# A two-layer hybrid attention encoder on one core: steps recorded and sorted by a list pass in the kernel, one set of places, and float32 value products in runs

## The chip, the core and the metric

The kernel runs on one core of one Trainium2 chip. The core has five engines, each with a queue of its own that runs in order: TensorE (PE in the profile, with its weight loads as PEld), VectorE (DVE), ScalarE (ACT), GpSimd (POOL) and SyncE (SP), which here issues nearly all transfers. They meet through semaphores. Working memory is SBUF (128 partitions), matmuls write the eight banks of PSUM, and tensors lie in HBM. The metric is the device time of one execution in microseconds (us); less is better.

## The reference, cut to what matters

One sequence of 1,024 tokens with 1,024 features, float32, goes through two layers. Each layer has four attention groups side by side, a joint output projection and an MLP:

```python
for l in range(DEPTH):                                  # DEPTH = 2
    h = rms_norm(x, norm1_g[l])
    proj = h @ w_in[l]
    ...
    y_a = mla_mixer(...)     # 4 heads, latent, dense, 96-wide scores
    y_b = diff_mixer(...)    # 4 heads, softmax(s0) - lam * softmax(s1), dense
    y_c = swa_mixer(...)     # 4 heads, +-128 band with a sink
    y_d = na_mixer(...)      # 4 heads, 2-D neighbourhood on a 64-wide grid, bias
    mix = jnp.concatenate([rms_norm(y_a, ...), y_b, rms_norm(y_c, ...), rms_norm(y_d, ...)], axis=-1)
    x = x + mix @ w_out[l]
    h = rms_norm(x, norm2_g[l])
    x = x + jnp.square(jax.nn.relu(h @ w_up[l])) @ w_down[l]
return rms_norm(x, final_norm_g)
```

## The kernel before

Activations are kept transposed (features on partitions, tokens along the free axis). A product in float32 accuracy is made of three passes of the type float32r: a value is split into a high and a low part (`split`: ACT copies the high part, DVE subtracts it), and `passes` (L222, L223, L224) multiplies high by high, high by low and low by high, 512 columns each. The MLP uses a seven-product scheme for 2 x 2 blocks, so that its matmul count is 7/8 of the plain one.

**One layer, in order.** (1) `several` projects the first tiles of group B, then the second wave; the evacuations rotate (rope), split and store queries, keys and values in HBM (`emit_parts`, `to_values`). (2) Group B's dense attention (`attn_b`, `dense`, `softmax`) runs on 128 queries at a time: scores in two halves of 512 keys (L810), a reduction by DVE that negates and takes the minimum (L812), the exponential by ACT (L815). The second softmax is scaled by ACT (L898) and added by POOL (L190, `p<-p`). The result is transposed by PE in blocks of 128 x 128 (L846) and copied out of PSUM as a split pair: ACT writes `pth` (L196), DVE writes `ptl` (L190). The value product then takes values stored as 64 high and 64 low columns, and multiplies them with `pth` and with `ptl` (L834, L835), 256 queries wide; `pv_out` adds the two halves. Meanwhile the other projections are woven in. (3) Groups D and C (`attn_d`, `attn_c`, `banded`: L982 scores, L991 transposes, L1003 and L1004 value products) run head by head, with the latent up-projections of group A (`latent_up`) woven in. (4) Group A (`attn_a`, `dense`), with a first part of the output projection woven in. (5) The rest of the output projection, then `mlp_up` and `mlp_down`. In between, `tails` holds the short chains that end a head: reciprocal, transpose to rows, store to HBM, a broadcast load back (`rz`), a multiplication.

**What sets the order.** In attention the order of a queue comes from the framework's scheduler, which goes by the order of the code and by priorities (`weave`, `high_priority`); in the MLP PE's order is that of the code. Memory comes from pools with so many buffers per tag: `stack` tiles (queries and keys of a head, L810 and L982) share 8 places with the residual `x`, the bias has 1, values have 2. PSUM banks are divided anew for attention (mm 2, tr 2, sb 3, pv 1), the output projection and the MLP.

Of the kernel before, what the change touches and what calls it, by code (L numbers as in the profile page):

```python
# [14 lines left out]
F = mybir.dt.float32  # L15
# [85 lines left out]
def layout(i):  # L101

    def padded(a, axis):
# [9 lines left out]
    wo = i["w_out"].reshape(n, 8, P, DM)[:, [2, 3, 6, 7, 4, 5, 0, 1]].reshape(n, DM, DM)  # L113
# [23 lines left out]
        + [col(i["out_g_" + s]) for s in ("mla", "swa", "na")]  # L137
# [9 lines left out]

class Trunk:
    def __init__(self, ctx, tc, d, out):
        self.ctx, self.tc, self.nc, self.d, self.out = ctx, tc, tc.nc, d, out  # L150
        self.ahead, self.tails = 4, deque()
        pool = lambda **k: ctx.enter_context(tc.tile_pool(**k))
        self.const = pool(name="const", bufs=1)
        self.xp = pool(name="xp", bufs=8)
        self.big = pool(name="big", bufs=16)
        self.wp = pool(name="wp", bufs=3)
        self.cp = pool(name="cols", bufs=2)
        self.dram = pool(name="dram", bufs=1, space=bass.MemoryType.DRAM)


# [10 lines left out]
    @contextmanager  # L171
    def banks(self, **n):

        self.phase = getattr(self, "phase", 0) + 1
        with self.tc.tile_pool(name=f"ps{self.phase}", bufs=1, space=bass.MemoryType.PSUM,
                               reuse_waits="tile") as self.psum:
            self.nbanks = n
            yield

    def bank(self, tag, shape=(P, 512)):  # L180
        return self.psum.tile(list(shape), F, tag=tag, bufs=self.nbanks[tag], name=tag)
# [87 lines left out]
    def rows_of(self, col, grid=False):  # L269
# [6 lines left out]
        dr = self.dram.tile([n, P], F, tag="rows", bufs=4, name="drows")  # L276
        if grid:
            flat = dr.rearrange("a b -> (a b)").rearrange("(r b c) -> b r c", r=16, b=8)
            self.store(flat, sb.rearrange("b (r c) -> b r c", r=16))
# [23 lines left out]
    def setup(self):  # L303
        nc, d = self.nc, self.d
        tile = lambda shape, name, dt=F: self.const.tile(shape, dt, name=name)
# [75 lines left out]
    def attention(self, l):  # L381
        nc, tc, d = self.nc, self.tc, self.d
        rb = self.rb
        sbuf = lambda name, side="left": tc.tile_pool(name=f"{name}{l}", bufs=1, reuse_waits="tile", side=side)
        w_in = lambda t: d["w_in"][l, t]
        dr = lambda shape, name: self.dram.tile(shape, F, tag=name, bufs=1, name=name)
# [3 lines left out]
        qb, kb, vb = dr([2, 2, 4, 16, 2, S], "qb"), dr([2, 2, 4, 16, 2, S], "kb"), dr([4, P, 8, P], "vb")  # L390
# [1108 lines left out]
```

## Time and profile before

| | us |
|---|---|
| median of 3 runs | 2693.91 |
| lowest, highest | 2693.65, 2694.74 |
| the profiled execution | 2692.41 |
| its span, first to last instruction | 2690.6 |
| granted TensorE clock, mean | 0.971 of full |

The profile is of one execution. Its page gives the busy time of each engine; a group's row gives line, engine, operation, tiles and shapes, count, busy time and mean nanoseconds of one, then the engine's idle time ahead of it and what ended that. A view by windows cuts the span into stretches, and the chain of waits follows the last instruction back to what released it. A matmul's row lasts from its entry to the modelled end of its way through the array, so rows overlap. A plain float32 matmul stands as two records (40 of L299 in the program, 80 in the trace).

### The profile page before, as it was taken

What the parts mean: (1) busy time and instruction counts of PE and PEld (TensorE: products, weight loads), DVE (VectorE), ACT (ScalarE), POOL (GpSimd) and SP (SyncE); (2) the same over time, 40 slices, a digit from 0 to 9 for tenths busy, and PEclk for the clock granted to TensorE, in tenths of its full rate; (3) what the DMA queues carried; (4) which work ended last, traced back from release to release, by engine and by line L of the source; (5) the groups of instructions that cost most, each with busy time, mean ns of one, the idle gap of its engine ahead of it and who ended that gap; (6) DMA issues with size and microseconds to landing.
All of it is one profiled execution on the core that took longest, in us unless ns stands there. A gap on an engine that the chain in (4) does not pass through costs nothing.

```text
span 2690.6 us, 36835 instructions
## 1 busy us (share of the span) xinstructions
PE 2545.8 (95%) x12296; PEld 2107.6 (78%) x12296; DVE 2014.2 (75%) x3827; ACT 1442.9 (54%) x2601; POOL 496.9 (18%) x306
## 2 busy tenths in 40 slices
PE   8989988999899999999999999789998999999997
PEld 7778876787778887888877788678887788778886
DVE  6777867774977778888668777677749677788886
ACT  4667757664534444444437777576635344444444
POOL 2555642201000000000035556331010000000000
PEclk9999989999999999999999999889999999999998
DMA  5533598322144447444244446962221444664431
GB/s 169 177 106 123 160 282 254 83 88 60 51 154 143 161 162 269 146 141 141 96 136 140 121 118 174 306 200 70 70 71 61 152 152 151 227 221 150 132 102 63
DMA packets 186927, 389.15 MB, mean 145 GB/s; under 512 B 23712, under 2 KB 26736, under 8 KB 186736
## 3 DMA queue, kind: packets, MB, share of 16 engines
q1 hardware_dynamic: 172912, 361.62, 43.7%
q10 hardware_dynamic: 13824, 25.17, 2.6%
q8 instruction: 97, 1.59, 0.2%
q14 instruction: 94, 0.77, 0.1%
HBM read 263.29 MB, written 123.41 MB: 144 GB/s over the span
## 4 chain that ended last, share of the span: by engine, by line
PE 74%; DVE 12%; DMA 6%; ACT 4%; issue 3%; POOL 1%; SPq 0%; DVEq 0%; ACTq 0%; POOLq 0%
PE u L222 8%; PE u L224 8%; PE u L223 8%; PE mm L222 5%; PE mm L223 5%; PE mm L224 5%; PE p L222 5%; PE p L223 5%; PE p L224 5%; PE sb L810 3%; PE tr L846 2%; DVE p L812 2%; DVE part L190 2%; PE pv L835 2%; PE pv L834 2%
## 5 line engine op out<-in xcount | busy, mean ns | idle before, releaser
L196 ACT ACTIVATE wh<-raw 128x512 fp32r<-128x512 f32 x448 | 281.8, 630 | 595.9 <-PE u L223 336.0
L190 DVE TENSOR_TENSOR wl<-raw,wh 128x512 fp32r<-128x512 f32 x448 | 306.8, 685 | 76.9 <-ACT wh L196 75.6
L190 POOL TENSOR_TENSOR wl<-ws,wh 128x512 fp32r<-128x512 f32 (+1 forms) x112 | 146.5, 1310 | 1107.0 <-DMA saved<-x 664.1
L224 PE MATMUL u<-far,wl 128*128 128x512 f32 x768 | 302.4, 394 | 6.2 <-DVE wl L190 6.0
L222 PE MATMUL u<-far,wh 128*128 128x512 f32 x768 | 302.4, 394 | 3.3 <-ACT ev L1251 2.1
L223 PE MATMUL u<-far,wh 128*128 128x512 f32 x768 | 301.8, 393 | 0.9 <-DVE far L190 0.9
L190 DVE TENSOR_TENSOR ptl<-tr,pth 128x512 fp32r<-128x512 f32 (+2 forms) x384 | 238.3, 629 | 67.5 <-ACT pth L196 65.8
L815 ACT ACTIVATE p<-p,nm 128x1024 f32<-128x1024 f32 x192 | 220.1, 1147 | 91.1 <-DVE nm L812 89.6
L196 ACT ACTIVATE pth<-tr 128x512 fp32r<-128x512 f32 (+2 forms) x384 | 204.9, 546 | 104.4 <-PE tr L846 55.8
L222 PE MATMUL p<-far,wh 128*128 128x512 f32 x640 | 251.2, 393 | 2.6 <-DVE ev L190 2.6
L224 PE MATMUL p<-far,wl 128*128 128x512 f32 x640 | 250.0, 391 | 2.9 <-DVE wl L190 2.9
L223 PE MATMUL p<-far,wh 128*128 128x512 f32 x640 | 250.3, 391 | 0.0
L810 PE MATMUL sb<-stack 96*128 96x512 f32 x640 | 217.6, 421 | 18.8 <-DVE nm L812 17.8
L190 POOL TENSOR_TENSOR p<-p 128x1024 f32<-128x1024 f32 x64 | 154.0, 2410 | 141.4 <-ACT p L898 132.1
L190 DVE TENSOR_TENSOR raw<-raw 128x512 f32<-128x512 f32 x256 | 174.6, 686 | 6.7 <-DMA raw<-in_w_up 2.0
L224 PEld LDWEIGHTS u<-far,wl 128*128 128x128 f32 x768 | 145.8, 190 | 38.4 <-DVE wl L190 7.9
L222 PEld LDWEIGHTS u<-far,wh 128*128 128x128 f32 x768 | 146.1, 190 | 35.3 <-ACT ev L1251 2.9
L223 PEld LDWEIGHTS u<-far,wh 128*128 128x128 f32 x768 | 145.8, 190 | 31.9 <-DVE far L190 1.6
L222 PE MATMUL mm<-xh,wh 128*128 128x512 f32 x416 | 168.9, 406 | 1.3 <-DVE part L190 0.7
L812 DVE CUSTOM_DVE_ANT_0 p<-sb,zero,nm 128x512 f32<-128x512 f32 x192 | 142.4, 742 | 32.2 <-PE sb L810 28.6
L224 PE MATMUL mm<-xh,wl 128*128 128x512 f32 x416 | 166.5, 400 | 0.0
L223 PE MATMUL mm<-xl,wh 128*128 128x512 f32 x416 | 166.4, 400 | 0.0
(245 smaller groups left out, 5993.1 us busy)
## 6 DMA issues: line engine op xcount, KB each, us to landing
act<-acts SPq DMA_DIRECT2D x224, 256.0 KB
raw<-in_w_up SPq DMA_DIRECT2D x128, 256.0 KB
acts<-ev SPq DMA_DIRECT2D x128, 256.0 KB
raw<-in_w_down SPq DMA_DIRECT2D x128, 256.0 KB
acts<-ev ACTq DMA_DIRECT2D x96, 256.0 KB
ws<-in_w_in SPq DMA_DIRECT2D x76, 256.0 KB
rz<-drows SPq DMA_DIRECT2D x40, 256.0 KB
stack<-kd SPq DMA_DIRECT2D x32, 256.0 KB
```

The costliest lines, as they stand in the source:

```text
L190: (eng or self.nc.vector).tensor_tensor(out=out, in0=a, in1=b, op=op)
L196: nc.scalar.activation(hi, src, AF.Copy)
L222: mm(ps, w[0], x[0][:, sl], start=start, stop=False)
L223: mm(ps, w[0], x[1][:, sl], start=False, stop=False)
L224: mm(ps, w[1], x[0][:, sl], start=False, stop=stop)
L810: self.nc.tensor.matmul(ps, q[:, qt * P:(qt + 1) * P], k[:, sl], start=i == 0, stop=i == len(passes) - 1)
L812: self.nc.vector.tensor_tensor_reduce(out=p[:, sl], in0=ps, in1=self.zero[:, 0:1].bitcast(F).broadcast_to([P, 512]), scale=-scale, scalar= ...
L815: self.nc.scalar.activation(p, p, AF.Exp, bias=nm[:, 1:2], scale=-1.0, accum_out=z)
L834: nc.tensor.matmul(out, v[:, kt], h[:, sl], start=kt == 0, stop=False)
L835: nc.tensor.matmul(out, v[:, kt], lo[:, sl], start=False, stop=kt == 7)
L846: nc.tensor.transpose(t[:, k * 256 + i * P:k * 256 + (i + 1) * P], p[:, (j * 2 + k) * P:(j * 2 + k + 1) * P], self.ident)
```

## The change

Four things change together.

**Recording and sorting.** The kernel's `nc` is now a `Plan`: each call is recorded as a `Step`, with the tiles that it reads and writes as `View`s of `Cell`s. A stage's steps get a rank by a table (`SPAN`), spread over a stretch from start to end; `order` then walks all five queues with a price for each step (`price`), takes on each queue the ready step of lowest rank whose tiles find a place (`grant`, `place`), and `emit` issues all steps in that order, with the framework's order switched off on every engine. So all instructions have one source line, L648.

**One set of places.** SBUF is 40 places of 1,024 columns, 19 of 512, and small ones; PSUM is 8 banks. Any tile takes any free place of its size, under a cap per tag: stack 12, bias 3, values 5, transposed tiles 8, and for banks mm 8, tr 3, sb 4, pv 2.

**Value products in float32.** Values are stored as 64 plain columns (half the bytes). The transposed block is copied once, unsplit, into `pt`: by ACT in group B, by ACT and DVE in turn in D, C and A. The product is a float32 matmul with 64 columns of weights. In `dense` the two key blocks of a pair go to partitions 0 to 63 and 64 to 127 of the bank, and `pv_out` adds them; in `banded` the two go to the two heads of a pair, which now run side by side, and one copy evacuates both. The products of a block are one unit (`together`), issued as a run. Group C's heads are paired differently, and the weights' rows are laid out to suit.

**Group B's difference** is one DVE instruction instead of one by ACT and one by POOL. The first wave's evacuations read PSUM without a copy by ACT.

The diff, cut to what the prediction speaks of:

```diff
+class Plan:
+    def order(self):
...
+            for s in pick.steps:
+                free[n] = self.issue(s, max(t, free[n]))
...
+        return sorted(out, key=lambda s: (s.start, s.n))
...
+    def place(self, c, t):
+        k, coming = c.kind, self.coming[c.kind]
+        rank = bisect.bisect_left(coming[c.tag], c.rank)
+        if rank >= c.cap - self.live[k, c.tag]:
+            return False
...
+    PLACES = {"pair": 40, "half": 19, "row": 3, "col": 30, "bank": 8}
...
+    def emit(self):
+        real = lambda v: v.real() if isinstance(v, View) else v
+        steps = self.plan.order()
+        for c in self.plan.cells:
+            c.home = self.home
+        with self.tc.manual_schedule(engines={q.engine.engine for q in self.plan.queues.values()}):
+            for s in steps:
+                getattr(s.eng.engine, s.op)(*[real(a) for a in s.args], **{k: real(a) for k, a in s.kw.items()})
...
-    EV = (.5, .5, .7, 1)
-    EARLY, RC, RA, LA = 4, (8, 1), (3, 1), 0
+    SPAN = {"open": (0, 60), "b1": (62, 95), "lat": (95, 130), "pd": (130, 210), "pc": (210, 300), "b": (65, 300),
+            "d": (300, 400), "up": (300, 370), "c": (305, 405), "a": (405, 510), "mb": (330, 335), "md": (405, 410),
+            "mc": (415, 420), "ma": (515, 520), "o1": (505, 530), "o2": (530, 600), "mlp": (600, 1220)}
+    LAYER, SOON = 1250, 20
+    BANKS = {"mm": 8, "tr": 3, "sb": 4, "pv": 2}
...
     def to_values(self, dst, tag="mm"):
...
-            nc.scalar.activation(v[..., 0:64], src, AF.Copy)
-            self.tt(v[..., 64:128], src, v.bitcast(F)[..., 0:64], ALU.subtract)
...
+            nc.scalar.activation(v.rearrange("p (h k d) -> p h k d", h=2, k=4),
+                                 ps.rearrange("p (k h d) -> p h k d", k=4, h=2), AF.Copy)
...
-    def transposed(self, w):
-        return [self.ap.tile([P, 512], R, tag=n, bufs=3, name=n)[:, :w] for n in ("pth", "ptl")]
+    def transposed(self, ps):
+        t = self.place.tile([P, 512], F, tag="pt", bufs=self.NT, name="pt")[:, :ps.shape[1]]
+        if self.turns[0]:
+            self.nc.vector.tensor_copy(t, ps)
+        else:
+            self.nc.scalar.activation(t, ps, AF.Copy)
+        self.turns = self.turns[::-1]
+        return t
...
-                nc.tensor.matmul(out, v[:, kt], h[:, sl], start=kt == 0, stop=False)
-                nc.tensor.matmul(out, v[:, kt], lo[:, sl], start=False, stop=kt == 7)
...
+            with self.plan.together():
+                for n, j in enumerate((3, 2, 1, 0)):
+                    for k in range(2):
+                        nc.tensor.matmul(out[k * 64:(k + 1) * 64], v[:, j * 2 + k], pts[j][:, k * 256:k * 256 + 256],
+                                         start=n == 0, stop=n == 3)
...
-                nc.scalar.activation(ps[1], ps[1], AF.Copy, scale=c)
-                self.tt(ps[0], ps[0], ps[1], ALU.add, nc.gpsimd)
+                nc.vector.scalar_tensor_tensor(out=ps[0], in0=ps[1], scalar=c, in1=ps[0], op0=ALU.mult, op1=ALU.add)
...
+        def products(pv, half, kbs):
+            with self.plan.together():
+                for kb in kbs:
+                    pts, i0, i1 = done[kb]
+                    q0, q1 = max(i0, half * 4), min(i1, half * 4 + 3) + 1
+                    for r, v, pt in zip(heads, vs, pts):
+                        mm(pv[r, (q0 - half * 4) * P:(q1 - half * 4) * P], v[:, kb],
+                           pt[:, (q0 - i0) * P:(q1 - i0) * P], start=False, stop=kb == 2 + 3 * half)
```

How it moves instructions, at two places. First PE in group A of the first layer (`sb` and the later `bank` rows with `stack` are scores, `ident,p` transposes, `pv` or `pt,v` value products; xN means N in a row). Before:

```order
L834 MATMUL pv<-pth,v 128x256
L810 MATMUL sb<-stack 128x512 x3
L835 MATMUL pv<-ptl,v 128x256
L834 MATMUL pv<-pth,v 128x256
L835 MATMUL pv<-ptl,v 128x256
L846 MATMUL tr<-ident,p 128x128 x4
L810 MATMUL sb<-stack 128x512 x3
L834 MATMUL pv<-pth,v 128x256
L835 MATMUL pv<-ptl,v 128x256
```

The change, same engine and group:

```order
L648 MATMUL bank_107<-stack 128x512 x3
L648 MATMUL bank_103<-stack 128x512 x3
L648 MATMUL bank_105<-ident,p 128x128 x2
L648 MATMUL bank_102<-ident,p 128x128 x2
L648 MATMUL bank_101<-pt,v 64x256 x8
L648 MATMUL bank_105<-ident,p 128x128 x2
L648 MATMUL bank_102<-ident,p 128x128 x2
L648 MATMUL bank_104<-stack 128x512 x3
```

A block's value products stood in pairs between transposes and scores, each behind its own split; now eight of one block stand in a run, some steps after their transposes.

Second, SP from group C's first key store on, ahead of the band stage (groups D and C) of the first layer: `kd`, `qd` and `vd` are group D's keys, queries and values in HBM, `kc` and `qc` group C's keys and queries, `rq`, `rkv` and `latp` group A's latent tiles. Before:

```order
L169 DMA kc<-both 64x2x512 x2
L162 DMA stack<-kd 64x1024 x2
L162 DMA stack<-qd 64x1024
L162 DMA bias<-in_bias 128x768
L162 DMA stack<-kd 64x1024
L162 DMA stack<-qd 64x1024
L162 DMA stack<-kd 64x1024
L162 DMA rq<-drows 128x1024
L162 DMA rkv<-drows 128x1024
L162 DMA latp<-lat 128x1024 x2
```

The change:

```order
L648 DMA kc_126<-both 64x2x512 x2
L648 DMA v<-vd_124 128x512
L648 DMA stack<-kd_123 64x1024 x2
L648 DMA v<-vd_124 128x512
L648 DMA tabc<-in_c 128x1024
L648 DMA tabs<-in_s 128x1024
L648 DMA ws<-in_w_lat 128x512
L648 DMA stack<-qc_125 64x1024 x2
L648 DMA kc_126<-both 64x2x512 x2
L648 DMA stack<-qc_125 64x1024 x2
L648 DMA mask<-in_swa 128x384
L648 DMA rq<-drows_134 128x1024
```

Before, the loads of group D's later heads stood here, and group C's came behind the latent tiles. Now group D's first pair is complete here, group C's queries come next, and group D's second pair stands behind the latent tiles. From this store to the last load of group A's first head 31 MB pass through SP's queue before, and 30 MB now.

More of the change, by code (lines that the diff above doesn't have):

```diff
@@ L867, in dense @@
             step(job, j)
-        product(*ready.pop(0))
+        while runs:
+            products()
         yield True
```

1020 lines of the change are left out of this document (685 added, 335 removed).

## The prediction, made before the changed kernel ran

> **What bounds the kernel now.** I read the page's totals first, then one stretch in which TensorE (PE) runs undisturbed, then the same view cut into stages, then the chain of waits inside the worst stage.
>
> ```profile
> span 2690.6 us, 36835 instructions
> ## 1 busy us (share of the span) xinstructions
> PE 2545.8 (95%) x12296; PEld 2107.6 (78%) x12296; DVE 2014.2 (75%) x3827; ACT 1442.9 (54%) x2601; POOL 496.9 (18%) x306
> ```
>
> PE looks 95% busy, but a matmul's row is its whole way through the array, and the next starts long before it ends. So busy time hides slack, and pace shows it:
>
> ```profile
> 1100.00:1200.00 100.00, 100.00 (x443) 82.84 (x442) 85.66 (x139) 44.21 (x74) 0.00 (x0) 1.00 0.46 140
> ```
>
> 443 matmuls of 512 columns in 100 us are 0.227 us each (0.226 to 0.227): the full pace. Starts in the timeline give the other prices:
>
> ```profile
> 612.51 0.28 PE L834 MATMUL pv<-pth,v 128*128 128x256 f32 x1
> 612.63 0.28 PE L835 MATMUL pv<-ptl,v 128*128 128x256 f32 x1
> 612.75 0.27 PE L846 MATMUL tr<-ident,p 128*128 128x128 f32 x1
> ...
> 186.35 1.04 PE L846 MATMUL tr<-ident,p 128*128 128x128 f32 x8
> 187.15 0.47 PE L810 MATMUL sb<-stack 96*128 96x512 f32 x1
> ```
>
> A split-float32 (fp32r) matmul of 256 columns takes 0.12 (612.51 to 612.63), a 384-column one 0.174 by interpolation (an estimate), a transpose 0.10 to 0.11 (8 from 186.35 to 187.15). Now the stages: two attentions (four rows each) and two MLPs. A row reads: stretch, length, PE busy (x matmuls), PEld, DVE, ACT, POOL, granted clock, DMA share, GB/s.
>
> ```profile
> 0.00:84.00 84.00, 74.35 (x326) 61.01 (x327) 54.72 (x70) 35.66 (x54) 24.82 (x22) 0.98 0.60 193
> 84.00:330.00 246.00, 234.29 (x1235) 195.58 (x1234) 190.20 (x474) 176.47 (x287) 141.29 (x80) 0.96 0.44 128
> 330.00:476.00 146.00, 125.79 (x668) 102.97 (x667) 99.90 (x263) 96.23 (x244) 53.06 (x33) 0.92 0.87 261
> 476.00:695.00 219.00, 210.75 (x1187) 177.10 (x1186) 148.06 (x305) 122.99 (x223) 28.67 (x21) 1.00 0.26 75
> 695.00:1338.00 643.00, 625.00 (x2722) 513.01 (x2721) 506.36 (x797) 286.45 (x486) 2.39 (x2) 0.99 0.46 149
> 1338.00:1414.00 76.00, 73.37 (x331) 60.75 (x330) 51.97 (x53) 29.04 (x46) 23.37 (x17) 0.96 0.50 146
> 1414.00:1650.00 236.00, 225.95 (x1199) 188.94 (x1198) 182.05 (x464) 173.26 (x282) 137.50 (x77) 0.97 0.42 124
> 1650.00:1804.00 154.00, 130.25 (x697) 109.56 (x696) 105.49 (x272) 98.98 (x250) 57.08 (x36) 0.89 0.87 260
> 1804.00:2026.00 222.00, 213.99 (x1193) 180.09 (x1193) 151.25 (x306) 123.60 (x223) 28.73 (x21) 0.99 0.24 71
> 2026.00:2690.60 664.60, 632.10 (x2753) 518.56 (x2751) 524.19 (x832) 300.23 (x517) 0.00 (x0) 0.98 0.44 143
> ```
>
> Each stage's matmuls, grouped by width and multiplied with these prices, are the time it would take at full pace. For 330 to 476, some 158 of 512 columns, 144 of 384, 110 of 256 and 254 short ones make 36 + 25 + 13 + 28 = 102 us, so 44 are lost. All stages in order lose 15, 28, 44, 20, then 30 in the MLP; 6, 26, 46, 21, then 48. Attention loses 107 and 99 of its 695 and 688 us; the whole needs 2,405 us of pace and loses 285. The band stage (groups D and C, from 330 and from 1650) is the worst by rate, and DMA says why:
>
> ```profile
> 352.27 9.05 DMA stack<-kd
> 361.39 9.95 DMA latp<-lat
> 371.41 8.90 DMA vc<-both
> 380.33 7.31 DMA qar<-both
> ```
>
> This chain is four transfers in a row, each ended by the next. With the DMA engines at 0.87 and 261 GB/s there, but at 0.44 in the stage ahead, the loads come in one bunch, after the work that could have covered them.
>
> **The change part by part.** The profiled execution took 2692.4 us, 1.8 around its span; the median shown is 2693.9. The sum is made against 2692.4.
>
> *Value products.* 1,344 fp32r products go (1,152 of 256 columns, 128 of 384, 64 of 128): 138 + 22 + 7 = 168 us. In their place stand 672 float32 ones with 64-column weights: 576 of 256 columns, 64 of 384, 32 of 128. The nearest float32 row:
>
> ```profile
> 35.76 1.95 PE L299 MATMUL mm<-ident,rs_r 128*128 128x128 f32 x16
> 37.46 0.48 PE L222 MATMUL pv<-xh,wh 128*128 128x512 f32 x1
> ```
>
> These are 8 instructions (each stands as two records), 1.70 us to the next start: 0.21 to 0.22 us for 128 columns, so 0.44 for 256 and 0.65 for 384. Alone the new products cost 576 x 0.44 + 64 x 0.65 + 32 x 0.22 = 302 us. They come in pairs on the two halves of the array's columns, and if the halves run together they cost 151. No row of before has two matmuls side by side, so the bounds are 151 and 302, that is -17 and +134 against 168. I take 151: the two of a pair share neither weights nor partitions of the bank, and while one half runs the second record of its product the other is free for the first of the next. The Trainium skill, TensorEngine Tiling (Array Packing), Overview, allows up to 2x for weights of at most 64 columns. Its TensorE: Matmul & The Clock Gate, Part 3, measured 2.38x with three column tiles, 79% of 3; at that share the products would cost 190 by estimate, 39 more. No run here shows either yet.
>
> *Changing the array's shape.* The new order has 96 runs of these products, so 192 changes. The nearest row is a transpose of narrow 8-column weights between wide matmuls:
>
> ```profile
> 631.45 0.27 PE L273 MATMUL mm<-ident,rz 128*8 128x128 f32 x1
> 631.47 0.48 PE L222 MATMUL mm<-mixh,wh 128*128 128x512 f32 x1
> 631.79 0.39 PE L223 MATMUL mm<-mixl,wh 128*128 128x512 f32 x1
> ```
>
> From 631.45 to 631.79 are 0.34, what a transpose and a matmul take anyway (0.11 + 0.23): no cost. A full drain would be 0.28 - 0.12 = 0.16 us (the row at 612.63 against its pace), 31 us in all. I take 8, nearer to the row. The Trainium skill, TensorEngine Tiling (Array Packing), Key Properties, says a change of tiling mode drains TensorE, which speaks for the 31; the row at 631.45 shows no drain.
>
> *Zeroing products.* 16 of 512 columns go: -4.
>
> *DVE, ACT, POOL.* The rows that go or are nearest:
>
> ```profile
> L190 DVE TENSOR_TENSOR ptl<-tr,pth 128x512 fp32r<-128x512 f32 x256 | 173.2, 685 | 43.0 <-ACT pth L196 42.2
> ...
> L196 ACT ACTIVATE pth<-tr 128x512 fp32r<-128x512 f32 x256 | 148.0, 590 | 59.5 <-PE tr L846 55.8 <-DVE ptl L190 1.8 <-PE pv L834 0.2
> ...
> L190 POOL TENSOR_TENSOR p<-p 128x1024 f32<-128x1024 f32 x64 | 154.0, 2410 | 141.4 <-ACT p L898 132.1
> L898 ACT ACTIVATE p<-p,cb 128x1024 f32<-128x1024 f32 x64 | 72.9, 1144 | 12.2 <-DVE cb L897 10.3 <-DVE cb L896 0.8 <-DVE rs_r L255 0.7
> L200 DVE SCALAR_TENSOR_TENSOR xl<-x,par,xh 128x1024 fp32r<-128x1024 f32 x16 | 24.4, 1529 | 7.6 <-ACT xh L199 7.6
> ```
>
> Each transposed tile was copied by ACT, then subtracted by DVE; now one copy does. In group B the weighted difference moves from ACT and POOL (1.14 + 2.41 us one behind the other) to one DVE pass of at most 1.53. DVE loses 128 subtractions of 0.685 a layer and the band's 64 shorter ones and gains 64 such copies (half of them shorter) and 32 passes: about -50 us a layer; ACT about -70, POOL -77. None of them bounds a stage now (DVE is at 190 of 246 in B), so I count this only where it shortens a chain. In B a row's way to the transposes drops from 3.6 to 1.5 us. If DVE did become late there, the scores' reductions on it would be late next, and through them the score banks.
>
> *Places and order.* Score tiles q and k had 8 places, shared with the residual; now 12 of their own; the bias goes from 1 place to 3, the values from 2 to 5 at half the bytes. So a load no longer waits for the head before it, and group C's loads come ahead of the latent tiles. SP's queue moves 30 MB from group C's first key store to the first head of A, before 31, and that stretch begins here and ends with the stage at 476:
>
> ```profile
> 346.88 1.24 SPq L169 DMA_DIRECT2D kc<-both  x2
> ```
>
> That is 129 us. At 261 GB/s for a share of 0.87, so 300 at full share, 30 MB are 100 us, and PE has 102 for the whole stage, so neither alone needs 146. I take the stage at 108, with 38 of its 44 given back, and 42 of the second layer's 46; the least is 0, the most all. B's stage gives back half, 14 and 13, because its chain is shorter. The last attention rows (20 and 21 lost) give 8 each. The head, the way into the MLP (its sums of squares stand where they stood), the turn from up to down and the last norm have the same steps in the same order: nothing, that is 15 + 6 + 30 + 48 stay.
>
> Sum: -17 + 8 - 4 - 80 - 27 - 16 = -136, so 2692.4 - 136 = **2556 us**.
>
> **The rivals.** *Everything comes back* (all 206 of attention's loss): 2692 - 17 + 8 - 4 - 206 = 2473. For it: DMA is idle at 0.21 to 0.44 around the band stage. Against: groups C, D and A need each other's tails (a reciprocal, its store, its spread), which no order removes.
>
> *The band stage stays bound by DMA.* Then its 80 stay: 2636. For it: the bytes hardly fall, 100 us of transfers and 102 of matmuls have to overlap nearly whole, and group A follows without the output projection beside it. Against: the new places let a load go as soon as its data is in HBM.
>
> *The halves do not run together:* +151, 2707, slower or at best the same. Against it: nothing shared in a pair; for it: no row shows it.
>
> *The queue locks up (the other side, slower).* One fixed order on SP, stores and loads mixed, every issue in its turn:
>
> ```profile
> SPq L162 <- DVE wl L190: 602.9, 208, 39.8
> ```
>
> SP already stands 603 us behind DVE alone (208 waits, the longest 39.8). If a store ahead of a stage's loads waits for a late transpose, the loads behind it start late, and each uncovered one costs 7 to 10 us (the four rows above) and a lower granted clock behind it (0.92 and 0.89 in the band stages). It decides from about 7 more such landings a layer: 68 us, the gain. At 10 a layer it is 2 x 90 - 136 = +44, 2736. For it: the order rests on prices, not on what happens. Against it: the scheduler of before orders by forecasts as well.
>
> **How the numbers follow.** Forecast as above: 0.56. All comes back 0.13; band stage stays 0.15 (both faster); halves apart 0.08; queue locks 0.08. A measurement of this kernel can't tell less than about 0.2% (5 us) from no change. Faster: 0.56 + 0.13 + 0.15 = 0.84; of the last two 0.03 fall within 0.2%, 0.13 are slower. The likeliest case alone spans 2510 to 2610 (a third of its 123 us of recovered loss either way, and the drains). For eight in ten the range reaches to 2480, most of the way to the full recovery, and to 2660, past the band stage that stays together with the drains (2636 + 23); the two cases above 2700 are left out.
>
> **What would show it.** Value products: start to start 0.22 us over a run of 8 (right), 0.44 (halves apart). A run's first start and the first after it: 0.1 to 0.16 late if the shape's change drains. Band stage: length near 108 and fewer transfers in a row in its chain, against 146 with DMA at 0.9. Attention to the first up product: 695 now, about 628 if right. MLP stages: 643 and 665 again; if they move by over 10 us, the steps that I left out were wrong. SP waits: the same total or less, and none over 40 us with PE idle behind it. The forecast is wrong if PE's matmuls, counted by stage at these prices, still lose over 80 us in either attention.

## The result, and the profile after

| | before | after |
|---|---|---|
| median of 4 runs, us | 2694.32 | 2625.57 |
| lowest, highest | 2693.65, 2697.03 | 2622.23, 2635.10 |
| the profiled execution | 2692.41 | 2626.60 |
| its span | 2690.6 | 2624.8 |

The changed kernel takes 0.9749 of the time, with a 95% interval of 0.9722 to 0.9775. It is faster, as forecast, and inside the range, but the gain is 69 us where 136 were forecast. A second set of runs gave 2626.52 for it. One execution in the study, of the experiment that delays the sums of squares in the MLP, was in a slow state (4999.83 us) and is left out of that experiment's median.

First the page's totals:

```profile
span 2624.8 us, 35143 instructions
## 1 busy us (share of the span) xinstructions
PE 2499.5 (95%) x12272; PEld 1983.3 (76%) x12272; DVE 1890.8 (72%) x3555; ACT 1276.9 (49%) x2369; POOL 361.9 (14%) x242
```

DVE, ACT and POOL are relieved by 123, 166 and 135 us, and the time falls by 69: most of that relief was not on the path. Now the view by windows, cut at the same stages as before (head, group B, groups D and C, group A with the output projection, MLP, and again):

```profile
0.00:81.00 81.00, 57.27 (x243) 46.57 (x244) 48.15 (x67) 28.35 (x40) 21.37 (x18) 0.89 0.49 163
81.00:353.00 272.00, 259.80 (x1342) 198.13 (x1341) 193.06 (x440) 147.03 (x259) 85.68 (x56) 0.97 0.41 121
353.00:478.00 125.00, 109.39 (x642) 78.03 (x641) 71.27 (x210) 77.46 (x211) 38.84 (x25) 0.95 0.87 243
478.00:689.00 211.00, 208.02 (x1179) 160.71 (x1178) 125.37 (x264) 103.16 (x182) 34.51 (x24) 0.98 0.29 86
689.00:1314.00 625.00, 617.97 (x2722) 509.53 (x2721) 502.43 (x793) 283.23 (x489) 2.57 (x2) 0.99 0.45 153
1314.00:1382.00 68.00, 52.70 (x244) 43.46 (x243) 41.03 (x47) 16.49 (x26) 20.04 (x13) 0.92 0.39 115
1382.00:1654.00 272.00, 260.00 (x1343) 197.86 (x1344) 193.89 (x442) 147.06 (x259) 86.02 (x56) 0.97 0.42 123
1654.00:1774.00 120.00, 106.29 (x643) 76.75 (x641) 71.30 (x209) 77.47 (x212) 38.30 (x25) 0.97 0.87 250
1774.00:1983.00 209.00, 206.22 (x1177) 159.75 (x1176) 125.50 (x264) 103.24 (x181) 34.58 (x24) 0.99 0.28 86
1983.00:2624.80 641.80, 621.79 (x2754) 512.50 (x2752) 518.80 (x828) 293.46 (x515) 0.00 (x0) 0.99 0.44 148
```

Lengths alone mislead here, because the list pass moved work between stages: the head now holds 243 matmuls where it held 326, and group B's stage 1,342 where it held 1,235. So I count as the prediction did: the matmuls of each stage times their full-pace prices, and what the stage lasts beyond that is its loss. Counted from the first matmul, in both layers together, in us:

| stage | loss before | loss after | change | forecast |
|---|---|---|---|---|
| head | 8.0 + 6.1 | 23.5 + 17.8 | +27 | 0 |
| group B | 28.3 + 25.5 | 32.9 + 32.3 | +11 | -27 |
| groups D and C (band) | 44.2 + 46.6 | 34.8 + 30.0 | -26 | -80 |
| group A, output projection | 20.0 + 21.3 | 14.4 + 12.7 | -14 | -16 |
| MLP with the end | 29.6 + 47.9 | 11.7 + 24.9 | -41 | 0 |
| value products and zeroing (pace) | | | -23 | -21 |
| changes of the array's shape | | | in B, band and A | +8 |

The sum is -66, the difference of the spans. Only two lines came near their forecast. Attention, for which the change was costed, gave 25 us in 1,376; the MLP, which was costed at nothing, gave 41.

The timeline of PE around one run of value products in the first group B:

```profile
106.68 0.40 PE L648 MATMUL bank<-xh,wl 128*128 128x512 f32 x1
107.00 1.95 PE L648 MATMUL bank<-pt,v 128*64 128x256 f32 x16
108.88 0.50 PE L648 MATMUL bank<-xh,wh 128*128 128x512 f32 x1
```

Eight products (16 records) take 1.88 us to the next start. Inside the run two records start 7 ns apart and the next two 209 ns later. A pair of products has four records, so it takes 0.432 us: 0.216 for a product, as in the sum. Eight of these are 1.73, so 0.15 are lost, 0.05 of it behind the first records and 0.10 at the way out. The way in costs 0.09 to 0.10 here; as a median over the 64 dense runs it is 0.09 behind a transpose and 0.18 behind a 512-column product.

What PE waits for, by the view of waits, in the head, in group B and in the band stage of the first layer:

```profile
PE bank L648 <- DVE part L648: 10.7, 1, 10.7
PE bank L648 <- ACT xh L648: 7.1, 1, 7.1
PE bank L648 <- DMA stack<-kb: 2.9, 1, 2.9
...
PE bank L648 <- DVE p L648: 9.4, 9, 2.6
...
PE bank L648 <- DMA stack<-kc: 5.7, 3, 3.7
PE bank L648 <- DMA latp<-lat: 3.2, 4, 1.4
PE bank L648 <- DVE part L648: 2.6, 4, 0.9
```

Each line gives total, times and longest. The head has one wait of 10.7 us for DVE; group B waits for `p`, the weighted difference that moved to DVE; the band stage waits 10 us for DMA.

### The profile page after: what moved, and what is told of

It is laid out like the page before. It is cut to its first block, busy times and chain, and to the rows that moved or that the text cites. A ratio compares the mean times of both kernels' runs of the same rounds, so it can differ in the third digit from the quotient of the medians.

```text
span 2624.8 us, 35143 instructions
## 1 busy us (share of the span) xinstructions
PE 2499.5 (95%) x12272; PEld 1983.3 (76%) x12272; DVE 1890.8 (72%) x3555; ACT 1276.9 (49%) x2369; POOL 361.9 (14%) x242
## 5 line engine op out<-in xcount | busy, mean ns | idle before, releaser
L648 PE MATMUL bank<-far,wh 128*128 128x512 f32 x2816 | 868.9, 390 | 0.5 <-ACT ev L648 0.5
L648 PEld LDWEIGHTS bank<-far,wh 128*128 128x128 f32 x2816 | 528.1, 188 | 111.2 <-ACT ev L648 1.3
L648 PE MATMUL bank<-far,wl 128*128 128x512 f32 x1408 | 548.1, 389 | 1.2 <-DVE wl L648 1.2
L648 ACT ACTIVATE p<-p,col 128x1024 f32<-128x1024 f32 (+2 forms) x320 | 294.1, 920 | 190.6 <-DVE col L648 189.7
L648 POOL TENSOR_TENSOR wl<-ws,wh 128x512 fp32r<-128x512 f32 (+1 forms) x112 | 158.0, 1417 | 1126.3 <-ACT wh L648 1065.3
L648 PEld LDWEIGHTS bank<-far,wl 128*128 128x128 f32 x1408 | 264.5, 188 | 57.5 <-DVE wl L648 2.5
L648 PE MATMUL bank<-stack 96*128 96x512 f32 (+2 forms) x896 | 275.5, 397 | 20.2 <-DMA stack<-kc 6.6
L648 PE MATMUL bank<-ident,p 128*128 128x128 f32 x1376 | 258.2, 280 | 30.1 <-DVE p L648 17.8
L648 DVE TENSOR_TENSOR x<-bank,x 128x512 f32<-128x512 f32 x240 | 165.2, 689 | 155.2 <-PE bank L648 154.5
L648 PE MATMUL bank<-xh,wh 128*128 128x512 f32 x608 | 258.3, 426 | 8.5 <-ACT xh L648 7.1
L648 PE MATMUL bank<-xh,wl 128*128 128x512 f32 x608 | 255.9, 422 | 0.4 <-POOL wl L648 0.4
L648 PE MATMUL bank<-xl,wh 128*128 128x512 f32 x608 | 255.7, 421 | 0.0
L648 PEld LDWEIGHTS bank<-ident,p 128*128 128x128 f32 x1376 | 173.4, 142 | 79.3 <-DVE p L648 24.2
L648 PEld LDWEIGHTS bank<-stack 96*128 96x128 f32 (+1 forms) x896 | 160.6, 194 | 60.6 <-DVE col L648 15.6
L648 ACT ACTIVATE pt<-bank 128x512 f32<-128x512 f32 (+2 forms) x256 | 139.8, 556 | 104.9 <-PE bank L648 101.1
L648 DVE CUSTOM_DVE_ANT_0 p<-bank,zero 128x512 f32<-128x512 f32 x192 | 131.6, 685 | 69.7 <-PE bank L648 66.1
L648 DVE TENSOR_TENSOR wl<-raw,wh 128x512 fp32r<-128x512 f32 x224 | 148.9, 686 | 36.6 <-ACT wh L648 36.6
L648 PE MATMUL bank<-pt,v 128*64 128x256 f32 (+2 forms) x1344 | 173.9, 399 | 0.0
L648 DVE CUSTOM_DVE_ANT_0 p<-bank,zero,col 128x512 f32<-128x512 f32 x192 | 144.0, 750 | 28.0 <-PE bank L648 7.0
L648 ACT ACTIVATE ev<-ev 128x512 f32<-128x512 f32 x128 | 80.5, 632 | 160.0 <-DVE ev L648 154.7
L648 PEld LDWEIGHTS bank<-xh,wh 128*128 128x128 f32 x608 | 118.7, 195 | 40.3 <-ACT xh L648 7.1
L648 ACT ACTIVATE wh<-raw 128x512 fp32r<-128x512 f32 x224 | 135.2, 621 | 26.2 <-ACT ev L648 10.5
```

Of the source, the lines that this page charges most:

```text
L648: getattr(s.eng.engine, s.op)(*[real(a) for a in s.args], **{k: real(a) for k, a in s.kw.items()})
```

## The experiments

Their times are to be compared with the changed kernel's 2625.6 and 2626.5; the kernel before took 2696 to 2701 beside them, and the ratios are to that. Losses, waits and clocks come from one profiled execution of each kernel.

### The changed kernel again

> The changed kernel again, as it stands, beside the next three and on their chip: 0.972 to 0.978 of the kernel before, and the yardstick for them.

2626.52 us, ratio 0.9715 [0.9695, 0.9734]. Stage losses moved by up to 4 us against the first profile without any edit, so a stage's difference below that tells nothing. (The next three, on that chip, are the copies by ACT, the products on the same columns and the fewer bytes; the others ran on other chips, so compare their ratios.)

### Value products on the same columns

```diff
-                        nc.tensor.matmul(out[k * 64:(k + 1) * 64], v[:, j * 2 + k], pts[j][:, k * 256:k * 256 + 256],
-                                         start=n == 0, stop=n == 3)
+                        nc.tensor.matmul(out[0:64], v[:, j * 2 + k], pts[j][:, k * 256:k * 256 + 256],
+                                         start=n == 0 and k == 0, stop=n == 3 and k == 1)
```

> The changed kernel, with the two products of a pair in the dense groups B and A on the same 64 columns of the array, accumulated into the same 64 partitions, instead of side by side; the order of all steps stays. Theory (side by side is what brings the products from 302 to 151 us): 512 products take 0.43 us in place of 0.216, and the time grows by 80 to 110 us against the control. Rival (the halves' pace comes from 64-column weights, not from running beside each other): within 10 us.

(To fit, `pv_out` now copies the one half and takes the larger of two equal values instead of adding.) 2713.77 us, ratio 1.0044 [1.0031, 1.0056]: 87 us slower than the control, and 0.4% slower than the kernel before. Its timeline:

```profile
105.19 3.67 PE L648 MATMUL bank<-pt,v 128*64 128x256 f32 x16
108.79 0.50 PE L648 MATMUL bank<-xh,wh 128*128 128x512 f32 x1
```

The same run now takes 3.60 us instead of 1.88: running side by side is worth a factor of two, and the whole gain of the change hangs on it.

### A product of zeros ahead of each run, or in its middle

```diff
+                    if n == 2:
+                        nc.tensor.matmul(out, self.zero, self.zero[:, 0:1].broadcast_to([P, 256]), start=False, stop=False)
```

(In the first of the two kernels the same product stands ahead of the run and opens the bank.)

> The changed kernel with one product more ahead of each of the 64 dense runs: a full-width fp32r product of zeros, 256 columns, which opens the bank; no change of the array's shape is added. Both theories: 64 x 0.12 = 8 us at most, 0 to 8 against the control. It is the yardstick for the next.

> The same product of zeros in the middle of each dense run instead of ahead of it: the array changes its shape twice more in each of 64 runs. Theory (a change out and in costs 0.2 to 0.28 us in all, as the starts around a run show): 13 to 18 us slower than with the product ahead of the run. Rival (the starts around a run are late for other reasons, a change is free): within 4 us of it.

2624.47 us ahead of the run, ratio 0.9721 [0.9697, 0.9745]; 2655.40 in its middle, 0.9834 [0.9814, 0.9854]. One run of the second kernel:

```profile
563.64 1.08 PE L648 MATMUL bank<-pt,v 128*64 128x256 f32 x8
564.65 0.38 PE L648 MATMUL bank<-zero 128*128 128x256 f32 x1
564.96 1.08 PE L648 MATMUL bank<-pt,v 128*64 128x256 f32 x8
565.98 0.66 PE L648 MATMUL bank<-ident,p 128*128 128x128 f32 x4
```

Four products are 0.86 at their pace and take 1.01; the product of zeros is 0.12 and takes 0.31. So this change out and in costs 0.15 + 0.19 = 0.34 us, 22 us over 64 runs. The measured 31 are more than theory said. Between the two profiled executions, 37 us apart, groups B and A lost 29 us more, the band stages, which have no such product, 12 more (37.5 and 36.0 against 30.0 and 31.2) and the heads 4 less; what the change itself does beyond its 22 us is not shown. With 0.24 to 0.34 for each of 96 runs, the changed kernel pays 23 to 33 us for its shape changes, some 9 in each of groups B, D with C, and A.

### The norm of the head earlier; copies by ACT; the values first

```diff
+            with self.plan.sooner(40):
                 acc = self.squares(self.x, self.place, "p", self.NP)
                 self.spread_here(rb, self.rstd_cols(acc, DM, self.ones[:, 0:1]))
                 tabs = self.table("32", rb, nc.vector)
```

> The changed kernel with one edit: in the head of each attention the sums of squares of the norm, their reciprocal roots and the rope tables get a rank 40 us earlier, so that they are sorted into the middle of the first wave of projections instead of its end. Theory (the place in the order is what the head loses): PE's idle stretch of 11 us ahead of the value transposes goes, the head's loss falls from 23.5 and 17.8 us to about 8 and 6, and the time from 2625.6 to 2598 to 2606. Rival (the evacuations that now read PSUM on DVE without a copy by ACT are what is late, wherever the norm stands): the idle stretch stays over 7 us and the time is within 6 us of 2625.6.

2623.83 us, ratio 0.9717 [0.9701, 0.9732], the same time. The wait for DVE's part fell from 10.7 to 6.2, and 2.8 of waiting for the sums came up earlier; the head lost 22.1 and 15.1. What the heads gave, 4 to 6 us, the band stage of the second layer lost again (40.0 instead of 31.5 in the control). The rival's stretch of over 7 us didn't stay either: both reasons were too simple.

```diff
+                raw = self.ptile()
                 for n in range(2):
-                    ev(n, b[n])
+                    sl = slice(n * 512, n * 512 + 512)
+                    nc.scalar.activation(raw[:, sl], b[n], AF.Copy)
+                    ev(n, raw[:, sl])
```

> The changed kernel with one edit: ACT again copies the first wave's six banks into a score tile each, and the evacuations read that copy, as in the kernel before. Theory (22 evacuation steps on DVE, 16 us in a row, keep six banks, and PE has nothing that it may start): the 10.7 us wait for DVE's part ahead of the value transposes falls below 4 us, the head's loss from 23.5 and 17.8 us to 10 to 16 and 6 to 12, and the time by 10 to 22 us against the control. Rival (the chain on DVE is as long with the copies, and the transposes come behind it anyway): the head stays within 4 us in each layer and the time within 6 us.

2640.59 us, ratio 0.9771 [0.9749, 0.9792]: slower. The wait for DVE's part was gone (0.3), and PE waited 9.4 for ACT's split at the same place instead; the head lost 21.4 and 17.2. The time was lost elsewhere, 10 us in group B and 12 in the second layer's band stage. The copies of the kernel before were not what kept its head short.

```diff
-            for ev, b in zip(evacs_b(0), banks):
+            for ev, b in list(zip(evacs_b(0), banks))[::-1]:
```

> The first experiment (the norm's reduction 40 us earlier) with one edit more: the values of the first wave are evacuated ahead of the keys and queries, so that their transposes need DVE only for two steps and not for 22. Theory (PE stands at the value transposes while the rope steps pass on DVE): the 6.2 us wait for DVE's part falls below 2, the head's loss from 22.1 and 15.1 us to 13 to 18 and 6 to 11, and the time by 6 to 14 us against the first experiment and the control. Rival (the evacuations end when they end, and what waits next is the load of the first scores' keys): the head stays within 3 us, and the wait for the keys' load grows from 2.3 to over 6.

2631.22 us, ratio 0.9754 [0.9730, 0.9778]. The rival was right, but for the tile: the head lost 18.9 and 14.2, and the wait is for queries, not keys. The waits in the first 84 us:

```profile
PE bank L648 <- DMA stack<-qb: 8.8, 1, 8.8
```

The wait for DVE's part had vanished, and the same length came back as a wait for the first scores' queries. Three edits had now moved one wait to three places.

### The second wave ahead of the first scores

```diff
-    SPAN = {"open": (0, 60), "b1": (62, 95), "lat": (95, 130), "pd": (130, 210), "pc": (210, 300), "b": (65, 300),
+    SPAN = {"open": (0, 60), "b1": (62, 78), "lat": (95, 130), "pd": (130, 210), "pc": (210, 300), "b": (78, 300),
```

> The changed kernel with one edit in the table of ranks: the second wave of projections is ranked 62 to 78 in place of 62 to 95, and group B's scores from 78 in place of 65, so that PE has the whole second wave ahead of the first score. Theory (the first scores stand too early, and PE waits in order for their loads): the waits for loads of keys and queries go, the first score stands near 92 us, the head's loss falls from 24 and 19 us to 15 to 20 and 11 to 15 (the wait for DVE's part stays), and the time by 6 to 16 us against the control. Rival (the transfers and the steps on DVE set the time at which group B can start, and what PE does ahead of it is missing as cover later): within 5 us.

> The same with the norm's reduction 40 us earlier and the values of the first wave evacuated ahead of keys and queries. Theory (the wait for DVE's part ahead of the value transposes and the early scores are two causes that only together leave PE without work): the head loses 7 to 12 and 5 to 9 us, as before the change, and the time falls by 16 to 30 us against the control, to 2594 to 2610. Rival (as with each edit alone, the wait moves on to the next load): the head loses over 16 and 12, and the time is within 8 us of the control.

(The second kernel also has the earlier norm and the values first.) 2615.79 us with the table alone, ratio 0.9692 [0.9659, 0.9724]; 2607.36 with all three, 0.9650 [0.9626, 0.9674]. The heads lose 19.4 and 13.2, then 11.0 and 4.4. The first 90 us of the second kernel, as a window:

```profile
0.00:90.00 90.00, 78.67 (x343) 64.67 (x344) 55.09 (x78) 32.89 (x48) 29.53 (x26) 0.96 0.55 178
```

Of its 343 matmuls 332 stand ahead of the first score at 88 us, as 328 did in the kernel before (241 in the changed one), and neither wait is left. Of the 26 us that the heads give back 19 show in the time. So there are two causes, and each hid behind the other: the first scores stood too early in PE's queue, and the norm and the values were late in DVE's.

### Group B's difference on ACT and POOL again

```diff
-                nc.vector.scalar_tensor_tensor(out=ps[0], in0=ps[1], scalar=c, in1=ps[0], op0=ALU.mult, op1=ALU.add)
+                nc.scalar.activation(ps[1], ps[1], AF.Copy, scale=c)
+                self.tt(ps[0], ps[0], ps[1], ALU.add, nc.gpsimd)
```

> The changed kernel with one edit: group B's weighted difference goes back to one instruction by ACT and one by POOL. Theory of the prediction (the shorter chain helps group B): the stage from the first to the last B score loses 10 to 14 us more in each layer, and the time is 2645 to 2655. Rival (with the difference on DVE, DVE is late for the transposes, 9.4 us in 9 waits of the first layer; PE had cover for the longer chain): the stage loses 5 to 9 us less, and the time is 2608 to 2616.

2628.81 us, ratio 0.9728 [0.9708, 0.9748]: no difference in all. But group B lost 22.6 and 23.9 instead of 29.6 to 32.9, so the prediction's reason (the shorter chain helps) was the wrong way round, and the band stage gave it back: 41.2 and 38.6. Its window, and below it the control's:

```profile
341.50:472.30 130.80, 112.67 (x639) 81.93 (x638) 71.29 (x207) 78.50 (x211) 41.56 (x27) 0.91 0.88 247
```

```profile
350.30:472.90 122.60, 106.16 (x640) 75.96 (x638) 69.94 (x208) 77.20 (x211) 38.87 (x25) 0.97 0.87 243
```

The same matmuls wait equally long (16 to 18 us by the view of waits), but the granted clock is 0.91 instead of 0.97: PE at half clock for 24 us instead of 7. The order need not be the cause: the profiled execution of this kernel was the slowest of its four (2633.60 us, the others 2621.66 to 2629.31), and the changed kernel itself had 14 us at half clock in this stage in its first profile and 7 in the control's.

> The same again with group B's difference back on ACT and POOL. Theory (group B gains 5 to 10 us a layer and keeps them): 8 to 20 us faster than without this edit. Rival (the band stage loses at a lower granted clock what group B gains, as in the two runs that had this edit): within 6 us, with a band stage of over 128 us and a granted clock of at most 0.92 there.

On top of the mended head the edit keeps its gain: 2598.39 us, ratio 0.9614 [0.9589, 0.9639], 9 us less than without it. Group B loses 27.9 and 26.1, and the band stage nothing more:

```profile
336.70:455.70 119.00, 105.44 (x637) 74.96 (x635) 67.83 (x206) 78.55 (x213) 42.12 (x27) 0.97 0.89 263
```

The rival falls, and this is the fastest version of the study, 27 us ahead of the changed kernel. What sets the granted clock of the band stage stays open: with the mended head alone it was 0.92 there (loss 33.9, 13.9 us of waits), with this edit 0.97 (loss 30.2).

### Fewer bytes in the band stage

One of three such edits (group D; the others are group C's keys and the latent tiles):

```diff
-                q, k, rows = self.stack(), [self.stack() for _ in range(2)], slice(j * 64, j * 64 + 64)
+                q, k, rows = self.stack(), [self.stack()] * 2, slice(j * 64, j * 64 + 64)
...
-                for i in range(2):
-                    self.load(k[1].bitcast(F)[i * 64:i * 64 + 64], kd[1, t, rows])
```

> The changed kernel with less to load in the band stage, some 4.5 MB of 28.6 a layer: the low halves of the keys of groups D and C and of the latent tiles are left out, and the high halves are multiplied in their place, so that every other instruction stays and the output is another. Theory (the band stage is bound by the transfers): its loss falls by 10 to 18 us in each layer, from 33 and 28, and the time by 20 to 36 against the control. Rival (it is bound by the chains of its heads, and DMA only looks full): 0 to 4 us a layer, at most 8 in all.

2612.82 us, ratio 0.9667 [0.9649, 0.9686]: 14 us faster, between the two. The band stages lost 26.7 and 25.1, 6 less each, and of PE's 10 us of waiting for DMA in the first one stayed 1.1. So the transfers are a part of what the band stage still loses, not most of it.

### What the MLP gained

```diff
-                    out = []
-                    for k in range(4):
-                        out.append(self.piece("act"))
+                    out = [t for i in range(2) for t in self.twin("raw")]
```

> The changed kernel with one edit: the activations that the down-projection loads take the places of the up-projection's weights (tag raw, 4 pairs) as they did in the kernel before, instead of 10 places of their own. Theory (own places are what the turn from up to down gained): the turn loses 6 to 9 us in each layer again (1 now), and the time is 2637 to 2643. Rival (the sorted order is what gained there): the turn stays below 3 us and the time within 4 us of 2625.6.

2625.78 us, ratio 0.9719 [0.9704, 0.9733], MLP losses 8.8 and 24.7: the places of their own gained nothing.

```diff
+        if self.code and q.name == "tensor":
+            if self.tail and self.tail not in s.before:
+                s.before.append(self.tail)
+                self.tail.after.append(s)
+            self.tail = s
```

> The changed kernel with one edit: within the MLP PE takes its steps in the order of the code, as in the kernel before; the other queues are sorted as now. Theory (PE's sorted order is what the way into the MLP gained): the first 60 us of the MLP lose 19 us again instead of 11, in both layers, and the time is 2640 to 2650. Rival (the order on DVE and ACT gained it, PE's does not matter): the entry stays within 3 us and the time within 6 us of 2625.6.

2638.35 us, ratio 0.9763 [0.9746, 0.9779]. 12 us slower, but the way into the MLP stayed: MLP losses 12.2 and 29.7. At least half of the cost stands in the second attention.

```diff
+            self.plan.gate = "vector", self.plan.steps[-1]
             acc = sums(1, (4, 5, 6, 7, 0, 1, 2, 3), acc)
+            self.plan.gate = None
```

> The experiment with PE in code order in the MLP, with one edit more: DVE and ACT take the sums of squares of the second half only behind the last split of the fourth operand, as in the kernel before. Theory (the sorted order had DVE finish the sums 10 us earlier, which the product of ones needs): PE waits 3 to 6 us ahead of that product again in each layer, the first 60 us of the MLP lose 15 to 19 us, and the time is 2642 to 2654. Rival (the way into the MLP gained from something else): the MLP loses no more than in the experiment with PE alone, 12 and 30, and the time is within 4 us of its 2638.

2638.68 us, ratio 0.9789 [0.9762, 0.9816], MLP losses 12.1 and 29.7, as without the gate. PE's wait ahead of the product of ones (which adds the squares up over the partitions) stayed 0.4, and the time is the rival's. But the gate did not make the sums late, so whether early sums are what the way in gained is not tested.

```diff
+                if not j:
+                    self.plan.gate = "sync", stored
                 bs = [self.twin("b") for m in M]
...
+                self.plan.gate = None
```

> The changed kernel with one edit: the down-projection's weights b and c and the second set of activations, of the first of its four steps, are loaded only behind the last store of the up-projection (now 12 to 18 us ahead of it). Theory (that the sorted queue issues these loads early is what the turn from up to down gained): the turn loses 4 to 10 us more in each layer, 8 to 20 us in all against the control. Rival (the loads have time to spare either way): within 4 us.

2652.11 us, ratio 0.9820 [0.9796, 0.9845]. MLP losses 22.1 and 36.6, 10 more in each layer. In the 70 us around the first layer's turn PE loses 10.2, against 1.4 in the changed kernel and 9.5 in the kernel before. SP's timeline at the turn, in the kernel before and in the changed one:

```profile
1000.64 1.76 SPq L162 DMA_DIRECT2D raw<-in_w_down  x4
...
1018.87 0.35 SPq L162 DMA_DIRECT2D raw<-in_w_down  x1
...
1020.23 0.99 SPq L162 DMA_DIRECT2D act<-acts  x2
```

```profile
986.43 2.25 SPq L648 DMA_DIRECT2D b<-in_w_down  x4
988.77 6.45 SPq L648 DMA_DIRECT2D c<-in_w_down  x8
```

The first down product comes at about 1017 before and 1002 after. Before, the weights went out until 1019, past the turn, mixed with five loads of activations (at 1002 to 1014), and more activations came behind them; now b and c are issued by 995, 7 us ahead of it. So the turn's gain needs these early loads. That they are all of it is not shown: PE's longest wait at the turn was for DVE's split of a weight before (3.0 us), and in the gated kernel for ACT's copy of loaded activations (6.8).

### Other prices for the list pass

```diff
-                t += 100
+                t += 170 if s.tiled else 150
...
-            begin = max(t + 1350, self.pipe)
+            begin = max(t + 1900, self.pipe)
```

> The changed kernel with other prices in the list pass: 0.15 and 0.17 us for a change of the array's shape instead of 0.10, 0.14 more for the weighted difference on DVE, and 0.55 us more to a transfer's landing with 15% more per byte; nothing else. Theory (the missing gain is lost to a forecast that is too bright: PE's queue holds items that are not ready): PE's waits for DVE's p and for DMA in groups B, D and C halve (18 and 13 us a layer now), and the time falls by 10 to 25 us against the control. Rival (the transfers and the chains bound these stages, whatever is foreseen): within 6 us.

> The same prices, with the norm's reduction 40 us earlier and group B's difference back on ACT and POOL. Theory (the edits add up once the order fits the prices): group B loses 22 instead of 31, the head 2 to 4 less, the band stage not more than in the control, and the time is 2596 to 2610, the fastest of all. Rival (what group B gives back, the band stage takes, because its transfers end when they end): 2615 to 2632.

2628.80 us, ratio 0.9747 [0.9727, 0.9767], and with two edits more 2630.55, 0.9751 [0.9734, 0.9767]. Both rivals' times came true; that transfers are the reason was not tested. Truer prices alone gain nothing. In the kernel with two edits more, group B and the head lose 2 to 6 us less a stage, and the band stages lose 41.4 and 40.9, at a granted clock of 0.91 and 0.90.

## Why the prediction was wrong

The step that failed is the one by which the new order gives back 107 us of waiting in group B and the band stage and leaves the head as it is: it gave 15 there, and the head lost 27 more. That the time still lies inside the range is luck: without the 41 us that the MLP gave, which the prediction put at nothing, it would be 2667, outside it. Term by term:

*Value products: right.* -23 with the zeroing against -21. The pair runs side by side at 0.216 us, and apart at 0.43. The Trainium skill, TensorEngine Tiling (Array Packing), Overview, allows up to 2x for such weights; the trace shows 2.0 inside a run (0.43 against 0.216). The 2.38x that the Trainium skill, TensorE: Matmul & The Clock Gate, Part 3, has for three column tiles is short of 3; no such shortfall shows with these two.

*Changing the shape: the term was mis-sized,* 23 to 33 us for 8. "From 631.45 to 631.79 are 0.34, ... no cost" took a product with 8-column weights as a row for this change; the runs with 64-column halves cost time where that row costs none. The loss is 0.15 us in a run and at its way out and 0.09 to 0.19 at its way in, so the prediction's bound of 31 lies inside what was measured, and the 8 that it took does not. By the Trainium skill, TensorEngine Tiling (Array Packing), Key Properties, a change of mode drains TensorE; the trace agrees with these 0.24 to 0.34 us.

*The band stage: mis-sized, and the largest miss.* "I take the stage at 108, with 38 of its 44 given back": it lasts 124 and 120 from the last B score to the first A score and gave back 26 for 80. Some 9 of the 54 missing are shape changes, and 13 came back when a sixth of the bytes went and PE's waits for DMA nearly vanished (10 us to 1.1 in the first layer, 7.6 to 0.5 in the second); what the other 32 are no run shows. In the first layer PE still waits 15 us there and has half clock for 14. That 100 us of transfers and 102 of matmuls "have to overlap nearly whole" was seen as a rival, and it was the better forecast of this stage.

*Group B: the step "because its chain is shorter" failed.* A single DVE pass put `p` behind DVE's other work: 9.4 us in 9 waits, against 2.2 in 3 with ACT and POOL. With ACT and POOL again the stage lost 6 to 10 us less a layer, and 9 us in all once the head was mended. The forecast -27 became +11, of which some 9 are shape changes.

*The head: "the same steps in the same order: nothing" failed,* +27. The steps had changed (no copy by ACT), and so had the order, which the list pass sets by the table. The timeline of PE shows the hole, and the window behind it the granted clock:

```profile
55.53 0.39 PE L648 MATMUL bank<-xh,wl 128*128 128x512 f32 x1
66.67 1.11 PE L648 MATMUL bank<-ident,part 128*128 128x128 f32 x4 [10.75 <-DVE part L648]
```

```profile
58.00:71.60 13.60, 4.93 (x16) 4.00 (x17) 11.63 (x18) 4.12 (x7) 1.08 (x1) 0.50 0.66 175
```

The 10.75 us of idle PE leave it at half clock until 71.6, 5 us beyond their end. The order, not the copies, was the cause: with the second wave first, the norm earlier and the values first the heads lose 15.4 together, as the 14.1 before.

*The MLP: the same step failed the other way,* -41. The prediction's own test ("if they move by over 10 us, the steps that I left out were wrong") says so. The turn gave about 8 us in each layer and needs the early loads. The way in gave some 8 in the first layer and 11 in the second, and its cause stays open: neither the places nor PE's order brought its loss back, and the gate on the sums did not make them late. The windows from the first up product to the end of the sums, before and now, show only what DVE was spared:

```profile
695.50:735.50 40.00, 32.31 (x141) 25.30 (x139) 39.30 (x65) 25.75 (x46) 0.00 (x0) 0.97 0.19 53
```

```profile
689.20:720.40 31.20, 30.84 (x141) 25.57 (x139) 30.61 (x50) 23.05 (x42) 0.00 (x0) 1.00 0.05 17
```

It is busy throughout in both, for 65 instructions and for 50; 8 of the 15 fewer are combinations of weights (`raw<-raw`, 12 and 4). That these are the cause was not tried.

*Group A: right in size,* -14 for -16, shape changes included; the prediction gave no reason for it, and no run tested one. SP's queue did not lock up: all its waits are 2,017 us where they were 2,088, and the longest grew only from 59.0 to 62.0, with under 1 us of idle PE behind it. (The 603 us of the prediction were one line of that view.) The forecast's own line for wrong, "still lose over 80 us in either attention", is met: 106 and 93.

## What to carry to other kernels

When a list pass takes over the order, no stage is "the same steps in the same order": cost every stage, those that the change does not name first. Where an idle engine waits in order, moving what it waits for moves the wait; look for the item that stands too early in its queue. A product that changes the array's shape needs runs long enough to pay for the way out and in.

## What the runs showed of the hardware

Two float32 products with 64-column weights on the two halves of the array's columns run fully side by side (0.216 us each for 256 columns, 0.43 apart), and each run of them costs 0.24 to 0.34 us beyond its products. In groups D and C the same matmuls with 16 to 18 us of waits ran at a granted clock of 0.91 in one profiled execution and 0.97 in another, which is 8 us of the stage. The two had different orders, but the same kernel too had 0.95 and 0.97 in two executions; no run here shows what decides it.
